# Order of work in a hybrid encoder block: value pairs ahead of their gate pairs, and three steps of background jobs moved by one tick

## The chip, the cores and the metric

One core of a Trainium2 chip runs the whole kernel in one launch. The metric is the device time in microseconds. TensorE (PE, with PEld for its weight loads), VectorE (DVE), ScalarE (ACT), GpSimd (POOL) and SyncE (SP) run side by side, each through its own list of instructions in order; they meet at semaphores. DMAs are issued from the queues of SP, ACT and POOL.

## The reference, cut to what matters

```python
h = rms_norm(x, pre_norm_w)                       # x: 2048 x 1024, float32
proj = h @ w_in                                   # 1024 x 7168
hy_in, hy_gate, sg_u, sg_v, sg_gate = split(proj)
x0, x1, v = split(short_conv_centred(hy_in, conv_w, conv_b))   # 3 taps
k = hyena_filter(...)
y_a = x0 * long_conv_bidir(v * x1, k, hyena_skip) * silu(hy_gate)   # by FFT in the reference
vn = layer_norm(sg_v, per head of 128) * sgu_norm_w + sgu_norm_b
mixed = einsum('hpq,bnqhd->bnphd', sgu_w, chunks(vn)) + sgu_b       # 8 heads, chunks of 128 rows
y_b = sg_u * mixed * silu(sg_gate)
out = x + rms_norm(concat(y_a, y_b) @ w_out, post_norm_w)
```

## The kernel before

**Foreground.** `Body.stream` computes the two projections as 72 "pairs" of 128-column blocks, each pair by a 2 x 2 block scheme with seven products (units 0 to 6) instead of eight. A unit is `product`: 12 matmuls of 128 x 128 by 512 columns into a PSUM bank `proj` (lines 304 to 306; operands are split into a high and a low part, so each product takes three matmuls). The moving operand of unit u is the tile `x_u` (buffer numbers in a listing tell the units apart), the weights are `wu`, made of `wraw` and `ws` by `prep_begin` (L606 to L614) and `prep_unit` (L631 to L637), one pair ahead. In the PE's order a pair runs unit 0, then units 5 and 6 of the pair before (`finish_pair`), then its own units 1 to 4. `snap` copies a bank to SBUF on ACT (`sn`, L648), `add` sums two banks' worth on DVE (L652).

**Kinds of pairs.** The rows are done in two halves (h = 0, 1). `self.order` is B(0) + U(0) + GV(0) + U(1) + GV(1) + B(1) + O(0) + O(1). A U pair makes two inputs of the long convolution, a G pair its gate and x0, a V pair (value pair) the `sg_v` columns of two heads, a B pair `sg_u` and its gate. There are 8 pairs of each kind, but 4 of V. O pairs are the output projection, 8 for each half of its inner dimension. GV(h) stands as G, G, V four times over. The stages, each with its own pool and its own background source, are: B(0); U(0); GV(0); U(1); GV(1) + B(1); O(0); O(1).

**Background.** What follows a projection is a generator, a "job": `go` runs it to its first `yield` and puts it on the list `active`; `tick` runs every job on the list by one step. `run` ticks at every second unit. A job that is put on the list during a tick gets its next step in that same tick, because the loop reaches the appended entry. `staggered` starts one job of a list per step.

- `u_job` (U pairs): two short convolutions (`conv`: ACT L879, DVE L880, L881), for h = 1 the product `ut` (DVE L914), then four `u1_job`s: four transposes of `ut` into bank `a` (PE L924), `uh`, `ul` (ACT L926, DVE L928), twelve matmuls into banks `b`, copies and two stores `AU<-ev` on the ACT queue each.
- `v_job` (V pairs, one for each of the two heads): loads `sw` and `bi` on the SP queue, one matmul with `ones` (PE L962, DVE L963) and two `mix_job`s: transposes of `v` (PE L980), per-row statistics and normalisation on DVE (L984, L985, L988, `vn` at L992) with a root on ACT (L987), then four matmuls with `sw` (PE L997) and the result back into `v` (DVE L1000). After that, for h = 1, one store `VM<-v` on SP; for h = 0 a load of `ug`, two products (DVE L1005) and two stores on SP.
- `o_job` (O(1) pairs, two output rows' blocks each): adds the part of O(0) (DVE L1129), sums squares on ACT (L1131, one instruction over 1024 columns into `part`), scales on DVE (L1132), root and reciprocal (L587, L589), final sum (DVE L1134) and the store on SP.
- `load_x` replaces the seven `x_u` at a change of half: one load on SP, casts on ACT (L558), subtractions on DVE (L559).

A scheduler of the framework sets the final order on each engine from the written order, the dependences and its own estimate of when each instruction can start; so a step that is written elsewhere comes out interleaved with the matmuls of other units.

Of the kernel before, what the change touches and what calls it, by code (L numbers as in the profile page):

```python
# [22 lines left out]
NJ = 16  # L23
# [102 lines left out]
class TakeU(Take):  # L126
# [11 lines left out]
    def c12(self, C, u2):  # L138
        self.b.add(self.r1[:, 9:17].rearrange("q j p -> q (j p)"), C, u2)
        self.b.go(self.b.u_job(self.h, self.c, self.r1, self.rv))  # L140
# [52 lines left out]
class TakeV(Take):  # L193
# [16 lines left out]

    def c12(self, C, u2):
        self.b.add(self.put(self.v0, 1), C, u2, self.view)
        for n, vr in enumerate((self.v0, self.v1)):
            self.b.go(self.b.v_job(self.h, self.c + n, vr))


class TakeO(Take):
# [28 lines left out]
class Body:  # L246
# [77 lines left out]
    def build(self):  # L324
        with ExitStack() as st:
            self.pp = st.enter_context(self.pool("pp", space=PSUM))
            self.dp = st.enter_context(self.pool("dp", space=DRAM))
            self.cp = st.enter_context(self.pool("cp"))
            dram = lambda n, s, dt=F32: self.dp.tile(s, dt, name=n)
            self.AU = dram("AU", [256, NJ, D])  # L330
            self.AK = dram("AK", [256, NJ, D])
            self.KF = dram("KF", [2, 32, 128, 512])
            self.BY = dram("BY", [256, NJ, D])
            self.XG = dram("XG", [NJ, 128, 8, 128])
            self.UG = dram("UG", [8, 128, D])
            self.VM = dram("VM", [8, 128, 8, 128])
            self.U0 = dram("U0", [8, 128, D])
            self.Y = dram("Y", [NJ, 128, 16, 128])
            self.WT = dram("WT", [2, 7, 128, 4, 512])
            self.PT = dram("PT", [NJ, 128, D])  # L340
            self.RB = dram("RB", [D])
            self.GD = dram("GD", [NJ, 128, 2, 128])
            self.XS = dram("XS", [7, 128, 4, 512])
            self.load_consts()
            self.xp = st.enter_context(self.pool("xp"))
            U = lambda h: [(h, "U", c, 8 + c, 16 + c) for c in range(8)]
            G = lambda h: [(h, "G", c, c, 24 + c) for c in range(8)]
            B = lambda h: [(h, "B", c, 48 + c, 32 + c) for c in range(8)]
            V = lambda h: [(h, "V", c, 40 + c, 41 + c) for c in range(0, 8, 2)]
            GV = lambda h: [p for n in range(4) for p in G(h)[2 * n:2 * n + 2] + V(h)[n:n + 1]]  # L350
            O = lambda r: [(r, "O", m, 2 * m, 2 * m + 1) for m in range(8)]
            self.order = B(0) + U(0) + GV(0) + U(1) + GV(1) + B(1) + O(0) + O(1)
            self.at, self.prev, self.to_spill = 0, None, []
            self.WS = {p[1:3]: dram(f"WS{p[1]}{p[2]}", [len(SPILL), 128, 2, 512]) for p in self.order[:28]}
            self.seen = set()
            self.wp = st.enter_context(self.pool("wp"))
            with self.pool("rp") as self.rp:
                with self.pool("xs") as xs:
                    self.x_phase(xs)
                with self.pool("sg") as self.fp:  # L360
                    self.nw_ = 3
                    with self.pool("mlp") as ml:
                        self.mlp(ml)
                    with self.pool("k1") as kp:
                        self.background(self.k1_jobs(kp), 1.4)
                        self.run(self.stream(8))
                        self.rest()
                with self.pool("fa") as self.fp:
                    self.nw_, self.nf = 4, 8
                    self.background(self.x_jobs(1), 0.25)  # L370
                    self.run(self.stream(8))
                    self.rest()
                self.nc.sync.dma_start(self.rc, self.RB.rearrange("(c q) -> q c", c=8))
                with self.pool("fd") as self.fp:
                    self.nw_, self.nf, self.nl = 5, 2, 3
                    self.background(self.kfft_jobs(), 0.85)
                    self.run(self.stream(12, 1))
                    self.rest()
                with self.pool("fb") as self.fp:
                    self.nw_, self.nf = 4, 3  # L380
                    self.f1 = self.fp.tile([128, 2, 2, 128], F32R, name="f1")
                    self.nc.gpsimd.dma_start(self.f1, self.i["c_f1"])
                    self.background(self.wo_jobs(), 0.32)
                    self.run(self.stream(8))
                    self.rest()
                with self.pool("fc") as self.fp:
                    self.nw_, self.nf, self.nl = 4, 6, 4
                    self.background(self.fft_jobs(), 1.0)
                    self.run(self.stream(20, "w0"))
                with self.pool("fo") as self.fp:  # L390
                    self.nw_ = 4
                    self.pw = self.fp.tile([128, D], F32, name="pw")
                    self.nc.scalar.dma_start(self.pw, self.i["post_norm_w"].partition_broadcast(128))
                    self.run(self.stream(8, "w1"))
                    self.run(self.stream(8))
                    self.drain()
# [499 lines left out]
    def u_job(self, h, c, r1, rv):  # L896
        nc = self.nc
        t1 = self.wide([128, 1024], "t1")
        if h:
            us = [self.fp.tile([128, 8, 2, 64], F32, name="ut", bufs=3) for _ in range(2)]  # L900
            for n in range(2):
                nc.sync.dma_start(us[n][:, :, 0], self.U0[c, :, n * 512:(n + 1) * 512].rearrange("q (j p) -> q j p", j=8))
        self.conv(t1, r1, 8 + c, h)
        yield
        t2 = self.wide([128, 1024], "t2")
        self.conv(t2, rv, 16 + c, h)
        if h == 0:
            nc.vector.tensor_tensor(t1, t1, t2, op=ALU.mult)
            nc.sync.dma_start(self.U0[c], t1)
            return  # L910
        for n in range(2):
            sl = slice(n * 512, n * 512 + 512)
            v1, v2 = [t[:, sl].rearrange("q (j p) -> q j p", j=8) for t in (t1, t2)]
            nc.vector.tensor_tensor(us[n][:, :, 1], v1, v2, op=ALU.mult)  # L914
        nc.vector.tensor_tensor(us[1][:, 7, 0, 63:64], self.fix[:, 8 + c:9 + c], self.fix[:, 16 + c:17 + c], op=ALU.mult)
        yield
        self.go(self.staggered([self.u1_job(c, n, us[n // 2]) for n in range(4)]))

    def u1_job(self, c, n, ut):
# [35 lines left out]
    def v_job(self, h, hd, vr):  # L955
        nc, i, fp = self.nc, self.i, self.fp
        sw = fp.tile([128, 128], F32, name="sw", bufs=2)
        nc.sync.dma_start(sw, i["sgu_w"][hd])
        bi = fp.tile([128, 128], F32, name="bi", bufs=2)
        nc.sync.dma_start(bi, i["sgu_b"][hd].partition_broadcast(128))  # L960
        ps = self.bank("a")
        nc.tensor.matmul(ps[:, :128], self.ones, sw, start=True, stop=True)  # L962
        nc.vector.scalar_tensor_tensor(bi, ps[:, :128], self.nb[:, hd:hd + 1], bi, op0=ALU.mult, op1=ALU.add)  # L963
        for n in range(2):
            self.go(self.mix_job(hd, n, vr, sw, bi))
            yield
        yield
        if h:
            nc.sync.dma_start(self.VM[hd], vr.rearrange("d b j p -> d b (j p)"))
            return  # L970
        ug = self.two("ug")
        nc.sync.dma_start(ug, self.UG[hd].rearrange("q (n c) -> q n c", n=2))
        for n in range(2):
            self.gated(h, hd, n, vr, ug[:, n])
# [149 lines left out]
    def o_job(self, j, y, part, done):  # L1124

        nc, fp = self.nc, self.fp
        xr = fp.tile([128, D], F32, name="xr", bufs=3)
        nc.sync.dma_start(xr, self.i["x"].rearrange("(p j) d -> j p d", j=NJ)[j])
        nc.vector.tensor_tensor(y[:, done:], y[:, done:], part[:, done:], op=ALU.add)  # L1129
        ss = fp.tile([128, 1], F32, name="ss", bufs=2)  # L1130
        nc.scalar.activation(part, y, AF.Square, accum_out=ss)  # L1131
        nc.vector.tensor_tensor(y, y, self.pw, op=ALU.mult)  # L1132
        rs = self.rstd(fp, ss)
        nc.vector.scalar_tensor_tensor(y, y, rs, xr, op0=ALU.mult, op1=ALU.add)  # L1134
        nc.sync.dma_start(self.out.rearrange("(p j) d -> j p d", j=NJ)[j], y)
        return
        yield


# [30 lines left out]
```

## Time and profile before

| | |
|---|---|
| median of 3 runs | 2086.94 us (2083.53 to 2091.46) |
| the profiled execution: its own time / its span | 2081.43 us / 2079.6 us |
| PE busy | 1907.2 us, 92% |
| DVE busy | 1347.8 us, 65% |
| ACT busy | 855.0 us, 41% |
| POOL busy | 446.3 us, 21% |
| granted TensorE clock, mean | 0.975 |
| HBM traffic | 250 GB/s over the span |

A row of a table by windows has the window in us from the span's start, its length, then busy us and instruction count of PE, PEld, DVE, ACT and POOL, the granted TensorE clock, the busy share of the DMA engines and GB/s. A row of the waits has engine, line, what released it, total us, times, longest us. A row of the timeline has start, us, engine, line, operation, out<-in, shapes, and in brackets the idle time before it with what ended it.

### The profile page before, as it was taken

What the parts mean: (1) busy time and instruction counts of PE and PEld (TensorE: products, weight loads), DVE (VectorE), ACT (ScalarE), POOL (GpSimd) and SP (SyncE); (2) the same over time, 40 slices, a digit from 0 to 9 for tenths busy, and PEclk for the clock granted to TensorE, in tenths of its full rate; (3) what the DMA queues carried; (4) which work ended last, traced back from release to release, by engine and by line L of the source; (5) the groups of instructions that cost most, each with busy time, mean ns of one, the idle gap of its engine ahead of it and who ended that gap; (6) DMA issues with size and microseconds to landing.
All of it is one profiled execution on the core that took longest, in us unless ns stands there. A gap on an engine that the chain in (4) does not pass through costs nothing. (4 is left out here: it accounts for less than half of the span.)

```text
span 2079.6 us, 23943 instructions
## 1 busy us (share of the span) xinstructions
PE 1907.2 (92%) x7832; PEld 1419.1 (68%) x7832; DVE 1347.8 (65%) x2070; ACT 855.0 (41%) x1538; POOL 446.3 (21%) x392
## 2 busy tenths in 40 slices
PE   4689999999999999888999999989999999999997
PEld 3465666777777766666777666656677777887776
DVE  6767878787655545655544888887773226436876
ACT  6344444565434443534444223322322224335443
POOL 3431322233222121111111101101011112323331
PEclk9899999999999999999999999989999999999999
DMA  8388777786779796897786888878978888536563
GB/s 265 110 265 268 238 261 253 227 274 230 247 258 297 259 315 208 327 274 236 256 276 194 294 271 265 282 237 274 302 244 307 282 269 282 194 102 243 192 212 132
DMA packets 330203, 515.89 MB, mean 248 GB/s; under 512 B 107451, under 2 KB 177339, under 8 KB 327359
## 3 DMA queue, kind: packets, MB, share of 16 engines
q1 hardware_dynamic: 263328, 439.58, 64.9%
q10 hardware_dynamic: 61856, 69.81, 9.8%
q0 software_dynamic: 4896, 4.98, 1.0%
q8 instruction: 62, 1.02, 0.2%
q14 instruction: 61, 0.50, 0.1%
HBM read 316.10 MB, written 204.48 MB: 250 GB/s over the span
## 5 line engine op out<-in xcount | busy, mean ns | idle before, releaser
L304 PE MATMUL proj<-x,wu 128*128 128x512 f32 x2016 | 834.9, 415 | 36.0 <-ACT sn L648 15.1
L305 PE MATMUL proj<-x,wu 128*128 128x512 f32 x2016 | 808.2, 401 | 10.6 <-DVE wu L637 8.8
L306 PE MATMUL proj<-x,wu 128*128 128x512 f32 x2016 | 806.6, 400 | 1.2 <-DVE x L559 0.6
L304 PEld LDWEIGHTS proj<-x,wu 128*128 128x128 f32 x2016 | 383.6, 190 | 146.2 <-issue 32.8
L637 POOL TENSOR_TENSOR wu<-wraw,wu 128x512 fp32r<-128x512 f32 x172 | 257.3, 1497 | 1038.1 <-ACT wu L635 855.5
L305 PEld LDWEIGHTS proj<-x,wu 128*128 128x128 f32 x2016 | 383.7, 190 | 113.3 <-issue 24.9
L306 PEld LDWEIGHTS proj<-x,wu 128*128 128x128 f32 x2016 | 383.2, 190 | 94.6 <-issue 12.7
L635 ACT CAST wu<-wraw 128x512 fp32r<-128x512 f32 x216 | 133.5, 619 | 281.6 <-PE proj L306 240.3
L637 DVE TENSOR_TENSOR wu<-ws,wu 128x512 fp32r<-128x512 f32 x176 | 129.7, 739 | 156.0 <-ACT wu L635 155.6
L635 ACT CAST wu<-ws 128x512 fp32r<-128x512 f32 x176 | 108.6, 620 | 220.3 <-PE proj L306 160.3
L648 ACT COPY sn<-proj 128x512 f32<-128x512 f32 x216 | 125.6, 581 | 108.4 <-PE proj L306 80.3
L614 POOL TENSOR_TENSOR ws<-wraw 128x512 f32<-128x512 f32 x44 | 79.0, 1795 | 174.5 <-DVE wu L637 111.7
L1073 DVE TENSOR_TENSOR pa<-b,k 64x512 f32<-64x512 f32 x128 | 87.4, 683 | 40.6 <-PE b L1070 29.8
L614 POOL TENSOR_TENSOR ws<-wraw,ws 128x512 f32<-128x512 f32 x44 | 59.5, 1353 | 223.4 <-DVE wu L637 210.1
L1073 DVE TENSOR_TENSOR pb<-b,k 64x512 f32<-64x512 f32 x128 | 88.8, 694 | 1.8
L614 DVE TENSOR_TENSOR ws<-wraw 128x512 f32<-128x512 f32 x44 | 39.6, 901 | 71.3 <-DMA wraw<-in_w_in_dram 39.2
L1082 PE MATMUL b<-pa,tb 128*128 128x512 f32 x128 | 71.7, 645 | 15.1 <-DVE pa L1077 5.5
L1084 ACT COPY ev<-b 128x512 f32<-128x512 f32 x64 | 37.4, 587 | 99.4 <-PE b L1082 88.8
L559 DVE TENSOR_TENSOR x<-x 128x1024 fp32r<-128x1024 f32 x42 | 56.3, 1381 | 19.2 <-ACT x L558 19.2
L1033 PE MATMUL b<-raw,tk 128*128 128x512 f32 x128 | 62.9, 612 | 5.5 <-issue 4.8
L862 PE MATMUL b<-s,ff 128*128 128x512 f32 x128 | 62.2, 603 | 4.4 <-ACT ev L864 2.9
L1070 PE MATMUL b<-raw,tu 128*128 128x512 f32 x128 | 63.2, 604 | 1.7 <-DMA raw<-AU 1.7
(170 smaller groups left out, 2230.5 us busy)
## 6 DMA issues: line engine op xcount, KB each, us to landing
wraw<-in_w_in_dram SPq DMA_DIRECT2D x84, 512.0 KB, 4.9
WSB<-wu SPq DMA_DIRECT2D x32, 512.0 KB, 4.8
dd<-in_c_dec_dram SPq DMA_DIRECT2D x32, 512.0 KB, 5.6
AK<-ev ACTq DMA_DIRECT2D x64, 256.0 KB, 4.5
WSU<-wu SPq DMA_DIRECT2D x32, 512.0 KB, 4.5
WSG<-wu SPq DMA_DIRECT2D x32, 512.0 KB, 5.0
raw<-AK SPq DMA_DIRECT2D x32, 512.0 KB, 6.9
KF<-ev ACTq DMA_DIRECT2D x32, 512.0 KB, 6.0
```

The source lines that it names most:

```text
L304: t.matmul(ps, sh, mh, start=first, stop=False, **kw)
L305: t.matmul(ps, sl, mh, start=False, stop=False, **kw)
L306: t.matmul(ps, sh, ml, start=False, stop=last, **kw)
L614: eng.tensor_tensor(t, x, y, op=op)
L635: nc.scalar.copy(w[:, 0], src[u])
L637: eng.tensor_tensor(w[:, 1], src[u], w[:, 0].bitcast(F32), op=ALU.subtract)
L648: self.nc.scalar.copy(s, ps)
L862: nc.tensor.matmul(ps, self.ff[:, d], s[d], start=True, stop=True)
L1033: nc.tensor.matmul(ps, tv[:, n], raw[:, n], start=True, stop=True)
L1070: nc.tensor.matmul(u, tv[0][:, n], raw[:, n], start=True, stop=True)
L1073: nc.vector.tensor_tensor(o, uu, kk, op=ALU.mult)
L1082: nc.tensor.matmul(ps, tv[1][:, n], prod[n], start=True, stop=True)
```

## The change

Four edits, all of order; each operation stays as it is.

1. GV(h) becomes V, G, G four times over: each value pair runs ahead of the two gate pairs that it followed.
2. A value pair's two `v_job`s are started through `staggered`, so the second head starts one step after the first; and `v_job` loses one empty `yield` ahead of its last step (the store of `VM`, or the load of `ug` and the products).
3. `u_job` gets one more `yield` ahead of the transposes of `ut`.
4. `o_job` gets a `yield` between the sum (L1129) and the sum of squares, except for the last two blocks of rows.

```diff
     def c12(self, C, u2):
         self.b.add(self.put(self.v0, 1), C, u2, self.view)
-        for n, vr in enumerate((self.v0, self.v1)):
-            self.b.go(self.b.v_job(self.h, self.c + n, vr))
+        self.b.go(self.b.staggered([self.b.v_job(self.h, self.c + n, vr) for n, vr in enumerate((self.v0, self.v1))]))
...
-            GV = lambda h: [p for n in range(4) for p in G(h)[2 * n:2 * n + 2] + V(h)[n:n + 1]]
+            GV = lambda h: [p for n in range(4) for p in V(h)[n:n + 1] + G(h)[2 * n:2 * n + 2]]
...
         nc.vector.tensor_tensor(us[1][:, 7, 0, 63:64], self.fix[:, 8 + c:9 + c], self.fix[:, 16 + c:17 + c], op=ALU.mult)
         yield
+        yield
         self.go(self.staggered([self.u1_job(c, n, us[n // 2]) for n in range(4)]))
...
         for n in range(2):
             self.go(self.mix_job(hd, n, vr, sw, bi))
             yield
-        yield
         if h:
...
         nc.vector.tensor_tensor(y[:, done:], y[:, done:], part[:, done:], op=ALU.add)
+        if j < NJ - 2:
+            yield
         ss = fp.tile([128, 1], F32, name="ss", bufs=2)
...
-        return
-        yield
```

Line numbers of the changed kernel are one lower than those of the kernel before over most of the file (the matmuls of a product are L303 to L305 there, the sum L651, `ut` L913, the split of `x` L558).

**The PE's order at the first turn of `u` in stage U(1).** The numbered `x` tiles tell the units: before, `x_6735` is that of unit 3 and `x_6759` that of unit 4. Before:

```order
L304 MATMUL proj<-x_6735,wu 128x512
L305 MATMUL proj<-x_6735,wu 128x512
L306 MATMUL proj<-x_6735,wu 128x512
L924 MATMUL a<-ident,ut 128x128 x8
L304 MATMUL proj<-x_6759,wu 128x512
L305 MATMUL proj<-x_6759,wu 128x512
L304 MATMUL b<-uh,f_6951 128x512
```

In the changed kernel `x_6720` is the tile of unit 0 and `x_6909` that of unit 5:

```order
L304 MATMUL proj<-x_6720,wu 128x512
L305 MATMUL proj<-x_6720,wu 128x512
L303 MATMUL proj<-x_6720,wu 128x512
L304 MATMUL proj<-x_6720,wu 128x512
L924 MATMUL a<-ident,ut 128x128 x8
L305 MATMUL proj<-x_6720,wu 128x512
L303 MATMUL b<-uh,f_6951 128x512
```

The eight transposes stood at the end of unit 3 of the next pair, 37 matmuls of `proj` behind the unit that ends the `u` pair, and stand now at the end of unit 0 of the pair after it, 60 matmuls behind. For the eight pairs of the stage this distance was 37, 50, 29, 46, 41, 46, 35, 36 matmuls and is now 60, 61, 49, 61, 49, 61, 50, 33.

**DVE's order at the first value pair of GV(0).** `v` are the value tiles of the two heads, `ws` a sum of weights for the next pair that reads the load `wraw`. Before:

```order
L652 TENSOR_TENSOR v_4702<-proj,sn 128x8x8x8
L637 TENSOR_TENSOR wu<-ws,wu 128x512 x2
L614 TENSOR_TENSOR ws<-wraw 128x512
L614 TENSOR_TENSOR ws<-ws,wraw 128x512
L652 TENSOR_TENSOR v_4623<-proj,sn 128x8x8x8
L963 SCALAR_TENSOR_TENSOR bi<-a,nb,bi 128x128
L984 BN_STATS bs<-a 128x6 x2
```

In the changed kernel:

```order
L651 TENSOR_TENSOR v_4330<-proj,sn 128x8x8x8
L636 TENSOR_TENSOR wu<-ws,wu 128x512 x2
L651 TENSOR_TENSOR v_4269<-proj,sn 128x8x8x8
L613 TENSOR_TENSOR ws<-wraw 128x512
L613 TENSOR_TENSOR ws<-ws,wraw 128x512
L983 BN_STATS bs<-a 128x6 x2
```

Here the last sum of `v`, for which the transposes wait, went from behind the two `ws` to ahead of them, and the statistics stand behind them. At the second, third and fourth value pair of GV(0) the two `ws` stand ahead of the last sum of `v` in the changed kernel; before, that was so at the first, second and third.

**DVE's order at the seam from GV(0) to U(1)**, where the seven `x` tiles are replaced. Before (`v_6679`, `v_6757` are the heads of the last value pair):

```order
L559 TENSOR_TENSOR x_6681<-x_6681 128x1024 x2
L652 TENSOR_TENSOR v_6757<-proj,sn 128x8x8x8
L963 SCALAR_TENSOR_TENSOR bi<-a,nb,bi 128x128
L559 TENSOR_TENSOR x_6705<-x_6705 128x1024 x2
L652 TENSOR_TENSOR v_6679<-proj,sn 128x8x8x8
L559 TENSOR_TENSOR x_6735<-x_6735 128x1024 x2
L984 BN_STATS bs<-a 128x6 x2
```

In the changed kernel (`r_6807`, `sg` and `t` belong to the last gate pair, `r_6992` to the first U pair):

```order
L558 TENSOR_TENSOR x_6809<-x_6809 128x1024 x2
L651 TENSOR_TENSOR r_6807<-proj,sn 128x512
L558 TENSOR_TENSOR x_6833<-x_6833 128x1024 x2
L879 SCALAR_TENSOR_TENSOR t<-r_6807,cw,t 128x1024
L558 TENSOR_TENSOR x_6863<-x_6863 128x1024 x2
L880 SCALAR_TENSOR_TENSOR t<-r_6807,cw,t 128x1024
L947 SCALAR_TENSOR_TENSOR sg<-sg,rc,t 128x1024
L558 TENSOR_TENSOR x_6888<-x_6888 128x1024 x2
L558 TENSOR_TENSOR x_6909<-x_6909 128x1024 x2
L558 TENSOR_TENSOR x_6939<-x_6939 128x1024 x2
L651 TENSOR_TENSOR r_6992<-proj,sn 128x512
```

The statistics and normalisation of two heads stood among the splits of `x` and went two pairs ahead; a gate pair's four instructions stand there instead, and all splits are now ahead of the first sum of U(1).

## The prediction

> **What bounds the kernel now.** I read the page first, then the windows by stage, then the waits of PE in each stage, then the timeline around the longest waits.
>
> ```profile
> span 2079.6 us, 23943 instructions
> PE 1907.2 (92%) x7832; PEld 1419.1 (68%) x7832; DVE 1347.8 (65%) x2070; ACT 855.0 (41%) x1538; POOL 446.3 (21%) x392
> ```
>
> PE is busy for 1907.2 of 2079.6 us. Order cannot remove a matmul, so what the change can win is part of the 172 us in which PE stands still, and time at a lower clock behind a stop. The windows below are GV(0), the seam with U(1), GV(1), the rest of that stage, and the two O stages.
>
> ```profile
> 530.00:857.00 327.00, 311.85 (x1294) 233.43 (x1294) 175.42 (x344) 146.01 (x273) 70.53 (x64) 0.98 0.83 274
> 857.00:1112.00 255.00, 224.56 (x1002) 180.01 (x1001) 143.45 (x221) 113.48 (x215) 39.16 (x41) 0.95 0.83 261
> 1112.00:1537.00 425.00, 405.16 (x1551) 270.21 (x1550) 332.53 (x579) 136.07 (x236) 50.35 (x45) 0.98 0.84 271
> 1747.00:2080.00 333.00, 308.99 (x1343) 252.09 (x1342) 214.97 (x259) 140.48 (x240) 95.29 (x62) 0.98 0.54 185
> ```
>
> The seam and U(1) have the most idle time for their length, 30.4 of 255 us, and the lowest clock, 0.95; the idle times of the others are 15.2, 19.8 and 24.0 us. The waits of PE say for what. Rows of 889 to 1142, then of 530 to 889, then of 1906 to 2080:
>
> ```profile
> PE a L924 <- DVE ut L914: 17.5, 7, 5.3
> PE b L304 <- ACT uh L926: 2.0, 1, 2.0
> PE b L306 <- DVE ul L928: 1.8, 2, 1.4
> PE proj L304 <- ACT sn L648: 0.6, 1, 0.6
> ...
> PE a L980 <- DVE v L652: 7.6, 3, 3.0
> PE b L997 <- DVE vn L992: 6.8, 2, 6.5
> ...
> PE proj L304 <- ACT sn L648: 5.8, 6, 1.0
> ```
>
> A stop costs twice. Below, a stop and the stretch behind it, three times, and the slow stretch behind the longest stop.
>
> ```profile
> 908.00:912.00 4.00, 0.00 (x0) 0.00 (x0) 3.96 (x4) 0.62 (x2) 1.55 (x1) 1.00 0.91 282
> 912.00:916.00 4.00, 3.39 (x13) 3.06 (x14) 3.27 (x6) 0.91 (x4) 1.37 (x3) 0.57 0.74 250
> ...
> 1034.00:1038.00 4.00, 1.54 (x13) 1.08 (x11) 4.00 (x5) 1.21 (x5) 1.42 (x3) 1.00 0.09 30
> 1038.00:1042.40 4.40, 4.40 (x14) 3.27 (x13) 2.20 (x4) 1.99 (x4) 0.23 (x1) 0.61 0.48 122
> ...
> 605.00:608.60 3.60, 1.61 (x10) 0.97 (x9) 2.69 (x6) 2.23 (x3) 0.66 (x1) 1.00 0.98 297
> 608.60:612.00 3.40, 3.40 (x12) 2.71 (x11) 1.11 (x8) 0.30 (x1) 0.00 (x0) 0.50 0.92 346
> ...
> 875.00:881.60 6.60, 3.06 (x13) 3.06 (x14) 6.19 (x17) 0.07 (x1) 1.82 (x1) 0.50 0.49 183
> ```
>
> After a stop of 2 us or more the clock is granted by half for 3.4 us: 4.0 us at 0.57, 4.4 at 0.61 and 3.4 at 0.50 each lose 1.7 us of matmul time.
>
> **The change part by part.**
>
> *Turns of `u` a step later.* The rows show the first wait, what DVE did before it, and how fast PE walks:
>
> ```profile
> 906.21 0.39 PE L306 MATMUL proj<-x,wu 128*128 128x512 f32 x1
> 906.43 0.39 PE L304 MATMUL proj<-x,wu 128*128 128x512 f32 x1
> 912.61 0.69 PE L924 MATMUL a<-ident,ut 128*128 128x128 f32 x2 [5.34 <-DVE ut L914]
> 949.34 1.00 PE L924 MATMUL a<-ident,ut 128*128 128x128 f32 x6 [4.60 <-DVE ut L914]
> 1037.15 0.55 PE L924 MATMUL a<-ident,ut 128*128 128x128 f32 x3 [2.46 <-DVE ut L914]
> 1121.89 0.66 PE L924 MATMUL a<-ident,ut 128*128 128x128 f32 x4 [0.92 <-DVE ut L914]
> ...
> 900.65 1.31 DVE L581 TENSOR_TENSOR t<-wo_raw 128x512 f32<-128x512 f32 x1 [7.91 <-DMA wo_raw<-in_w_out_dram]
> 908.35 2.29 DVE L881 SCALAR_TENSOR_TENSOR t<-r,cw,t 128x1024 f32<-128x1024 f32 x1
> 911.87 1.29 DVE L914 TENSOR_TENSOR ut<-t,t 128x512 f32<-128x512 f32 x2
> ...
> 907.70 1.86 POOL L637 TENSOR_TENSOR wu<-wraw,wu 128x512 fp32r<-128x512 f32 x1 [6.28 <-ACT wu L635]
> ...
> L880 DVE SCALAR_TENSOR_TENSOR t<-r,cw,t 128x1024 f32<-128x1024 f32 x6 | 7.7, 1284 | 6.1 <-ACT t L879 6.1
> ```
>
> A matmul of `proj` starts every 0.22 to 0.23 us. By the distances in the order (37, 50, 29, 46, 41, 46, 35, 36 matmuls before; 60, 61, 49, 61, 49, 61, 50, 33 now) the transposes come later by 5.2, 2.5, 4.5, 3.4, 1.8, 3.4, 3.4 and, at the last pair, -0.7 us of PE's own work. Of the waits 5.34, 4.60, 2.46 and 0.92 (first, second, fifth, eighth pair) this leaves 0.1, 2.1, 0.7 and 1.6, of the rest nothing: 4.5 of 17.5, so 13.0 us go. Of the stage's four slow stretches (the first and the third stand above, the others are at 950 and 1069) one stays, behind the 2.1: 3 x 1.7 = 5.1. Together 18.1 us. What is late next: `uh`, `ul` and `sn`, now 4.4 us together, stand right behind the transposes, and DVE in this stage is itself held by loads of `wo_raw` (7.91 us in one piece), which a faster PE does not bring forward. I let these waits double and take back 4: 14 us. Ends: 0, if all of it reappears there, and 18. The moved step issues eight stores `AU` per pair on the ACT queue; its DMAs go later behind the same copies, and nothing reads `AU` until the next stage. On SP and POOL it issues nothing. The slot of `ut` is held a step longer, but in the order its last transposes still stand ahead of the second next pair's loads.
>
> The operation L881 beside POOL's subtraction took 2.29 us, where L880 on the same shape takes 1.28. The Trainium skill, page SBUF — State Buffer, section Who interferes with whom, has it that a DVE instruction with two SBUF inputs and a reading GpSimd one exclude each other for the whole instruction; by it this one waits until 909.56 and lasts 2.49, near the 2.29 measured. By the row the term stays 14; by the rule, if every such pair met, it would be what the first rival gives.
>
> *Value pairs first, second head later: GV(0).* The last value pair's statistics collide at the seam with the splits of `x`; that is the 6.51 us below and the 6.6 us at half clock, 3.3 lost. In the new order a gate pair's work stands there. From the rows, a value pair costs DVE (21.9 + 16.0 + 11.9 + 9.8) / 4 = 14.9 us in these four groups, a gate pair (9.5 + 7.7) / 6 = 2.9 in its own product (L947) and the first of two like convolution steps (L880).
>
> ```profile
> 878.54 0.79 PE L997 MATMUL b<-sw,vn 128*128 128x128 f32 x2 [6.51 <-DVE vn L992]
> 891.46 1.40 PE L304 MATMUL proj<-x,wu 128*128 128x512 f32 x2 [2.40 <-DVE r L652]
> ...
> L992 DVE TENSOR_SCALAR vn<-a,mv,rs 128x128 f32<-128x128 f32 x64 | 21.9, 402 | 0.1
> L984 DVE BATCH_NORM_STATS2 bs<-a 128x6 f32<-128x128 f32 x64 | 16.0, 277 | 5.5 <-PE a L980 5.5
> L1000 DVE SCALAR_TENSOR_TENSOR v<-b,nw,bi 128x512 f32<-128x512 f32 x16 | 11.9, 741 | 4.9 <-PE b L997 4.8
> L985 DVE BATCH_NORM_AGGREGATE mv<-bs 128x2 f32<-128x6 f32 x64 | 9.8, 163 | 0.0
> L947 DVE SCALAR_TENSOR_TENSOR sg<-sg,rc,t 128x1024 f32<-128x1024 f32 x6 | 9.5, 1582 | 0.0
> ...
> 690.15 1.15 DVE L614 TENSOR_TENSOR ws<-wraw 128x512 f32<-128x512 f32 x1 [4.46 <-DMA wraw<-in_w_in_dram]
> 691.94 0.68 DVE L652 TENSOR_TENSOR v<-proj,sn 128x512 f32<-128x512 f32 x1
> ```
>
> So 6.5 + 3.3 = 9.8 us go; the 2.40 behind them I leave, since the splits still stand ahead of the first sum. But the same pair now meets the wait of the others: its sum of `v` stands behind a `ws` that waits for `wraw`, and costs 7.6 / 3 = 2.5 and 1.7 of clock, 4.2. The first value pair loses that wait (the sum is ahead of `ws` now), yet its statistics stand behind it, so `vn` is late by about as much: 0. The term is 9.8 - 4.2 = 5.6; ends -4.2 (the seam's wait only moves) and 9.8 + 2.4 + 3.7 - 4.2 = 11.7. The second head's loads `sw` and `bi` on SP come later with it and are read later; the last step of `v_job` comes a step earlier, its load of `ug` or store of `VM` too, ahead of which nothing on SP is due.
>
> *GV(1).* DVE is busy for 332.5 of 425 us, PE waits 19.8 in all, and the pairs are the same in another order. I take 0; the ends are the gain of an equal 5.6 and the second rival.
>
> *Sums of squares.* Their step is later in the written order, but on ACT the square stays right ahead of the `sn` copy for which PE waits 1.0 us a pair; the sum on DVE moves ahead of a 1.28 us operation in about half the pairs. 1.5 us, between 0 and all 5.8. No DMA but the output's store moves, and the last pair's chain is untouched.
>
> *Sum*: 14 + 5.6 + 0 + 1.5 = 21 us. Against the profiled execution, 2081.43 us (its span and 1.8 around it): 2060. That execution lies 5.5 below the median of the runs, 2086.94; against the median, 2066.
>
> **The rivals.** *The turns run into POOL.* With PE no longer standing, DVE's four operations of 1.28 us per pair and POOL's subtractions meet each time and take 2.3. That is 4 us a pair, more than the 3 us by which the transposes moved on average; the term of 14 falls to 0, and the time is 2086.94 - 7 = 2080. For it: the 2.29 at the first pair; against it: POOL has 39 us of work in 255.
>
> *The value pairs meet the transform in GV(1) (slower).* The second head's start falls into the same tick as the first head's second half, so DVE has two heads stacked at one place, while it is at 78% with the transform's products. If at each of the four value pairs PE waits for one head's statistics, 14.9 / 2 = 7.5 us and 1.7 of clock, that is 37 us: 2103. It decides from 21 / 4 = 5.3 us a pair; below, the kernel is still not slower. For it: the 6.51 at the seam, where DVE was loaded as much. Against: the work is the same as before, and PE has transform matmuls to run meanwhile.
>
> *It does not do what it says.* The scheduler places instructions by readiness, the second head starts about 20 matmuls later and the square not at all; if the seam's wait only moves, the turns alone count: 14 - 4.2 = 10, so 2077.
>
> **How the numbers follow.** No change and a change of 0.5%, 10.4 us, is about what a measurement of this kernel can tell apart: faster is below 2076.5, slower above 2097.4. The forecast, with its terms between half and their upper ends, 0.63, all of it faster. POOL 0.11 and the step without effect 0.12 are both within 0.5%. GV(1) 0.14: slower. The range: the upper ends together, 18 + 11.7 + 5.8 = 35.5, and the same again of the 5.6 in GV(1), give 2046; at the top both rivals within 0.5% and the median with no gain, 2087. Outside lie the slower rival and a little below. The likeliest case alone has 2048 to 2076.
>
> **What would show it.** Each step: PE's wait at L924 falls from 17.5 to about 4, and the clock of U(1) rises from 0.95; the 6.5 at L997 near the seam is gone; four waits of about 2.5 at L980 or L997 in GV(0) instead of three; the O stage's `sn` waits stay near 1.0. It is wrong if PE's idle time in U(1) stays at 30 us under other names, or if idle time in GV(1) rises above 30.

## The result and the profile after

The changed kernel took 2071.64 us (median of 6 runs, 2066.04 to 2078.3); the kernel before took 2084.71 us beside it (6 runs, 2082.41 to 2091.46). The ratio is 0.9936, with an interval of 0.9915 to 0.9956: 13 us faster, where 21 were forecast (2066 of 2086.94 is 0.990, outside the interval). Direction and range held; the size did not: the largest term was too large, and a stage that stood at nothing became longer. Of all executions here, two ran some 4% longer at a granted clock of 0.84 (2173.88 us of the squares alone, 2158.52 us of turns, heads and five slots); the ratios leave them out, the medians count them.

The profiled execution took 2072.21 us, its span 2070.2. Its page begins:

```profile
span 2070.2 us, 23947 instructions
PE 1904.2 (92%) x7832; PEld 1414.1 (68%) x7832; DVE 1345.9 (65%) x2070; ACT 857.4 (41%) x1540; POOL 452.0 (22%) x392
```

The work of each engine is what it was; the time came from PE standing still less. The windows of the stages (GV(0); the seam with U(1); GV(1); the O stages, all shifted a little, since the stages begin at other times now):

```profile
530.00:860.00 330.00, 317.58 (x1350) 238.46 (x1349) 187.83 (x402) 147.50 (x274) 71.00 (x64) 0.98 0.83 274
860.00:1098.00 238.00, 214.26 (x943) 169.41 (x942) 130.23 (x163) 110.02 (x210) 38.98 (x41) 0.97 0.86 273
1098.00:1531.00 433.00, 410.59 (x1594) 275.13 (x1592) 336.24 (x630) 143.42 (x246) 50.39 (x44) 0.98 0.83 265
1740.00:2070.00 330.00, 307.55 (x1337) 250.83 (x1335) 213.20 (x257) 138.76 (x237) 99.17 (x62) 0.99 0.54 185
```

In the seam and U(1) PE now stands still for 23.7 us (238.00 less 214.26) instead of 30.4, at a granted clock of 0.97 instead of 0.95; in GV(1) for 22.4 instead of 19.8. PE's waits, of U(1), of GV(0), of the seam alone (860 to 889.8) and of O(1):

```profile
PE b L303 <- ACT uh L926: 10.3, 6, 2.6
PE b L305 <- DVE ul L928: 3.3, 5, 1.0
PE a L924 <- DVE ut L913: 2.4, 1, 2.4
...
PE a L979 <- DVE v L651: 8.3, 3, 3.1
...
PE proj L303 <- ACT r L871: 4.1, 1, 4.1
PE proj L303 <- ACT sn L647: 2.7, 1, 2.7
...
PE proj L303 <- ACT sn L647: 3.7, 4, 1.0
```

The wait for `ut` is gone as forecast (17.5 to 2.4; of the 17.5, 0.9 stood at the start of GV(1), where the changed kernel has no such wait), but `uh` and `ul` hold PE for 13.6 us where they held it for 3.8. The 6.51 us at the normalised rows is gone from the seam, but the first products of U(1) wait there for `sn` and `r`, 6.8 us.

The table splits one profiled execution of each kernel at the first matmul of a stage (84 matmuls into `proj` make a pair; "seam" is the first pair of U(1)). In brackets stand PE's idle time and the time at half clock, in us; of the latter, half is lost. A kernel with "`x` kept" leaves out the exchange of `x` at the seam (see below). Each row is one execution, and a stage that no edit touches varies too: B(0) took 309.5 to 315.5 us in these fourteen.

| kernel | GV(0) | seam | rest of U(1) | GV(1) + B(1) | span |
|---|---|---|---|---|---|
| before | 327.4 (15.1/14) | 38.8 (9.3/10) | 215.3 (21.1/14) | 635.1 (20.2/14) | 2079.6 |
| after | 329.0 (12.4/10) | 29.7 (6.8/7) | 206.8 (16.9/7) | 641.6 (22.8/17) | 2070.2 |
| turns alone | 327.1 | 40.8 | 206.0 (14.8/11) | 636.2 | 2075.1 |
| order of pairs alone | 340.8 | 28.0 | 213.7 | 636.3 | 2085.0 |
| heads alone | 323.1 | 40.0 | 216.1 | 626.5 (15.5/3) | 2070.4 |
| squares alone | 325.1 | 38.5 | 219.3 | 634.0 | 2081.4 |
| after, five slots | 329.7 | 29.3 | 194.0 (5.5/0) | 636.5 | 2047.4 |
| before, five slots | 326.9 | 38.9 | 201.7 (12.1/7) | 632.1 | 2063.4 |
| turns and heads | 325.1 | 40.1 | 209.1 (16.2/14) | 626.4 | 2061.3 |
| after, value pairs first in GV(0) alone | 329.7 | 30.6 | 205.3 (14.8/10) | 627.9 (12.9/7) | 2055.2 |
| the same, five slots | 328.8 | 29.4 | 196.0 (6.4/3) | 626.9 | 2045.4 |
| turns and heads, five slots | 326.7 | 36.4 | 200.0 (10.6/3) | 631.2 | 2058.4 |
| before, `x` kept | 328.2 | 25.5 (0.0/0) | 221.2 | 632.9 | 2072.6 |
| after, `x` kept | 330.5 | 19.0 (0.0/0) | 203.0 | 637.5 | 2053.8 |

By this table the span's 9.4 us come from GV(0) with the seam -7.5, the rest of U(1) -8.5, GV(1) with B(1) +6.5, both O stages -0.9, and all stages ahead of GV(0) +0.9.

### The profile page after: what moved, and what is told of

It reads as the page before. It is cut to its first block, busy times and chain, and to the rows that moved or that the text cites. A ratio compares the mean times of both kernels' runs of the same rounds, so it can differ in the third digit from the quotient of the medians.

```text
span 2070.2 us, 23947 instructions
## 1 busy us (share of the span) xinstructions
PE 1904.2 (92%) x7832; PEld 1414.1 (68%) x7832; DVE 1345.9 (65%) x2070; ACT 857.4 (41%) x1540; POOL 452.0 (22%) x392
## 4 chain that ended last, share of the span: by engine, by line
PE 33%; DVE 8%; DMA 6%; issue 2%; ACT 1%; POOL 1%; SPq 0%; DVEq 0%; ACTq 0%; POOLq 0%
PE proj L305 8%; PE proj L304 8%; PE proj L303 8%; PE b L1081 3%; PE b L1107 2%; PE b L1069 2%; DMA x<-WT 1%; DVE pb L1072 1%; DVE pa L1072 1%; DMA wraw<-Y 1%; DMA WT<-t 1%; DVE x L558 1%; DVE pa L1076 1%; PE b L996 1%; DVE wu L636 1%
## 5 line engine op out<-in xcount | busy, mean ns | idle before, releaser
L303 PE MATMUL proj<-x,wu 128*128 128x512 f32 x2016 | 833.0, 414 | 35.7 <-ACT sn L647 13.2
L304 PE MATMUL proj<-x,wu 128*128 128x512 f32 x2016 | 810.8, 402 | 12.8 <-DVE wu L636 10.3
L305 PE MATMUL proj<-x,wu 128*128 128x512 f32 x2016 | 807.6, 401 | 1.1 <-DVE x L558 0.6
L636 POOL TENSOR_TENSOR wu<-wraw,wu 128x512 fp32r<-128x512 f32 x172 | 262.3, 1525 | 1047.5 <-ACT wu L634 819.1
L303 PEld LDWEIGHTS proj<-x,wu 128*128 128x128 f32 x2016 | 383.6, 190 | 143.6 <-issue 33.7
L305 PEld LDWEIGHTS proj<-x,wu 128*128 128x128 f32 x2016 | 383.4, 190 | 94.5 <-issue 13.5
L651 DVE TENSOR_TENSOR r<-proj,sn 128x512 f32<-128x512 f32 x64 | 43.8, 685 | 40.4 <-PE proj L305 39.6
```

The source lines that it names most:

```text
L303: t.matmul(ps, sh, mh, start=first, stop=False, **kw)
L304: t.matmul(ps, sl, mh, start=False, stop=False, **kw)
L305: t.matmul(ps, sh, ml, start=False, stop=last, **kw)
L636: eng.tensor_tensor(w[:, 1], src[u], w[:, 0].bitcast(F32), op=ALU.subtract)
```

## Each edit alone

Turns of `u` a step later, and nothing else:

```diff
         yield
+        yield
         self.go(self.staggered([self.u1_job(c, n, us[n // 2]) for n in range(4)]))
```

> The kernel before with the extra step ahead of the turns of u alone. Theory one (the account behind the forecast): PE's wait at L924 falls from 17.5 us to about 4, the waits for uh and ul grow to about 13, U(1) itself is about 9 us shorter, and of that 2 to 3 us come back at the start of GV(1), where the last turns now run: 5 to 9 us faster in all. Rival: the late turns delay the value pairs and the transform behind them, GV(1) is longer by what U(1) wins: within 2 us of the kernel before.

Measured: 2070.31 us against 2082.26, ratio 0.9950 (0.9930 to 0.9971). U(1) behind its first pair falls by 9.3 us, and PE waits there 3.5 us for `ut` and 9.9 for `uh` and `ul`. The first theory came, with a gain a little above its 5 to 9 us.

The order of the pairs, and nothing else:

```diff
-            GV = lambda h: [p for n in range(4) for p in G(h)[2 * n:2 * n + 2] + V(h)[n:n + 1]]
+            GV = lambda h: [p for n in range(4) for p in V(h)[n:n + 1] + G(h)[2 * n:2 * n + 2]]
```

> The kernel before with V ahead of its two G in both halves, alone. Theory one: the seam's wait of 6.5 us at L997 and its 3.3 us of slow clock go, the stage GV(0) is 2 to 4 us longer, GV(1) unchanged: 5 to 8 us faster. Rival: in GV(1) the value pairs lie two pairs earlier, where DVE is loaded by the transform, and GV(1) with B(1) takes 6 us more: within 3 us of the kernel before.

Measured: 2086.66 us, ratio 1.0019 (1.0001 to 1.0037): a little slower. The seam falls from 38.8 to 28.0 us, but GV(0) grows from 327.4 to 340.8; about 6.5 us of both are the last value pair's own matmuls, which went from the one to the other. Neither theory came: the gain did not, and GV(1) with B(1), 636.3 us, is not longer by the rival's 6 either.

The second head a step later (`staggered`, and the empty `yield` of `v_job` removed), and nothing else:

> The kernel before with the second head a step later and the empty step of a value pair's job gone, alone. Theory one: nothing that PE waits for moves by more than a microsecond, the time is within 3 us of the kernel before. Rival: the stacked heads are what lengthens GV(1) in the changed kernel: 4 to 7 us slower, in GV(1).

Measured: 2074.97 us, ratio 0.9971 (0.9956 to 0.9986). GV(0) loses 4.3 us, GV(1) with B(1) loses 8.6. Neither theory came: one had no change, the other a slower GV(1).

The squares a step later, and nothing else:

> The kernel before with the step ahead of the sums of squares alone. Theory one: the six waits of 1.0 us for sn in O(1) fall to 5.4 in all, as in the changed kernel: 0 to 1 us faster, which these runs cannot tell from nothing. Rival: the trace of the changed kernel hides a gain of some us by another cause; then 3 us or more.

Measured: 2082.32 us, ratio 1.0005 (0.9988 to 1.0023): no change clear of the noise. The waits of O(1) changed as in the changed kernel: `sn` fell, and the next one took most of it. Waits of before and of this kernel from 1906 to the end:

```profile
PE proj L304 <- ACT sn L648: 5.8, 6, 1.0
PE proj L305 <- DVE wu L637: 1.9, 1, 1.9
...
PE proj L304 <- ACT sn L648: 3.7, 4, 1.0
PE proj L305 <- DVE wu L637: 3.4, 3, 1.9
```

The sum of both is 7.7 us before and 7.1 here. Of the four edits two pay, one pays nothing, and the one that stands first in the change, the order of pairs, costs when it is alone; the four ratios multiply to 0.9945, and 0.9936 was measured for all together.

## Where the gain of the turns went: slots

PE waits in U(1) for `uh`, a copy on ACT. The question is what ACT waits for. ACT's waits of the changed kernel in U(1), DVE's there, and two of ACT's copies from the timeline:

```profile
ACT uh L926 <- DMA WT<-t: 8.6, 4, 4.5
ACT uh L926 <- DVE t L580: 4.5, 2, 3.3
...
DVE t L580 <- DMA WT<-t: 15.4, 6, 4.1
...
DVE ul L928 <- DMA WT<-t: 9.2, 5, 3.8
...
1031.94 0.58 ACT L926 CAST uh<-a 128x512 fp32r<-128x512 f32 x1 [3.27 <-DVE t L580]
1090.05 0.59 ACT L926 CAST uh<-a 128x512 fp32r<-128x512 f32 x1 [4.50 <-DMA WT<-t]
```

`uh` reads bank `a`, and neither `WT` nor `t` is its data. They are the tiles and stores of the weight job that runs in the background of this stage. Its differences `t` (L580) and `uh`, `ul` come from one ring of buffers (the helper `self.f`), and this stage gives the ring three. A copy to `uh` must wait until a store `WT<-t` has left the slot that it gets; `ul` waits for the same stores. In the changed kernel, `uh` falls on them more often: ACT's two waits come to 13.1 us, before to 4.7 (3.4 and 1.3). If that is so, more slots end it:

```diff
                 with self.pool("fb") as self.fp:
-                    self.nw_, self.nf = 4, 3
+                    self.nw_, self.nf = 4, 5
```

> The changed kernel with five instead of three slots of the pool's tile f in the stage U(1). Theory (slots): the 10.3 us for which PE waits for uh in the changed kernel come from ACT waiting for a slot that a tile t of the output weights' job still holds until its store WT has landed (8.6 and 4.5 us of ACT's waits); with five slots that wait falls below 4 us and U(1) behind its first pair gets 6 to 9 us shorter than the 206.8 of the changed kernel: about 0.35% faster than it. Rival (queue): ACT is late because its own list of casts and copies is long there; then the wait for uh stays at 8 to 11 us and the time with it.

Measured: 2057.49 us against 2079.74, ratio 0.9893 (0.9868 to 0.9918). U(1) behind its first pair takes 194.0 us instead of 206.8, with 5.5 us idle instead of 16.9. The stage is 12.8 us shorter, where 6 to 9 were expected; the theory of the slots came, the rival's wait of 8 to 11 us did not. PE's waits there, and the window of that stretch:

```profile
PE b L305 <- DVE ul L928: 2.3, 4, 1.4
PE a L924 <- DVE ut L913: 1.9, 1, 1.9
...
884.30:1078.30 194.00, 188.47 (x858) 148.37 (x856) 109.93 (x145) 94.94 (x185) 33.64 (x35) 1.00 0.90 282
```

No row is left for `uh`, and the granted clock is 1.00 over the stretch. `ul` on DVE still waits 7.4 us for stores `WT`, but PE feels only 2.3 of it.

The control is the kernel before with the same edit. There PE waited mostly for `ut`, so the slots should hardly matter:

> The kernel before with five slots in place of three, nothing else. Slot theory: the slots cost PE only what stands at `uh` and `ul`, 3.8 us of waits, since the wait for `ut` (16.5 us) comes first; 0 to 4 us, ratio 0.998 to 1.000. Rival, that more slots are worth the same without the later turns: 0.994 to 0.996.

Measured: 2071.08 us against 2082.59, ratio 0.9949 (0.9929 to 0.9969). This missed what I expected of the slots; the rival's number came. The slots alone are worth as much as the turns alone, and U(1) falls by 13.6 us. The waits of DVE before, in U(1), and the wait of PE for `ut`, before from 889 to 1111 and with five slots:

```profile
DVE t L581 <- DMA WT<-t: 9.6, 7, 2.3
...
PE a L924 <- DVE ut L914: 16.5, 6, 5.3
...
PE a L924 <- DVE ut L914: 12.9, 8, 5.1
```

```profile
944.91 1.09 PE L924 MATMUL a<-ident,ut 128*128 128x128 f32 x8 [1.69 <-DVE ut L914]
```

The first row was in the profile before, and I had not read it: DVE too waits for slots, 9.6 us, with `ut` queued behind it. With five slots that row is gone from DVE's waits, the 4.60 us at the second pair are 1.69, and PE has no row for `uh` and `ul` left. So the same ring held PE in two ways, by DVE ahead of `ut` and by `uh` and `ul`. The first way was the smaller part of the wait for `ut`: 3.6 of 16.5 us went with the slots, and at the first pair 5.11 of 5.34 us stayed. The later turns take away nearly all of that wait, whatever its cause, but they do not shorten the ring's hold: with them DVE's `t` waits 15.4 us for it, not 9.6, and `ul` 9.2, not 4.7. For the whole kernel the ratios multiply (0.9950 by 0.9949 by 0.9971 for the heads is 0.987, which is what the kernel with all three gave, below). In U(1) alone the two gains do not add up in full: 9.3 and 13.6 us apart, 15.3 to 21.3 in the three kernels that have both.

## The seam: the exchange of `x`

The sum had the stop at the seam go with the statistics. To see what the exchange of `x` itself costs, both kernels were run without it. The second half then runs on the first half's columns of `x`; its load, casts and splits are left out.

```diff
-                    self.run(self.stream(12, 1))
+                    self.run(self.stream(12))
```

> The kernel before without the exchange of the seven x tiles at the seam from GV(0) to U(1): the loads, casts and splits there are left out, and U(1) to GV(1) go on with the first half's rows. Theory (the seam is bound by the exchange: DMA at 1.0, DVE's 17.5 us of splits): even with the last value pair behind its gates the first pair of U(1) has less than 2 us of idle PE and takes 27 to 30 instead of 38.8 us. Rival (the value pair's own chain of statistics is too long for the matmuls around it): the wait of about 6 us at L997 stays.

> The changed kernel without the exchange of `x` at the seam: the second half runs on the first half's columns, so the loads, casts and subtractions of `x` there are left out. If the exchange of `x` holds the seam in the changed kernel too: the first pair of U(1) falls from 29.7 us (idle 6.8) to about 21, its waits for `sn` and `r` go, and the span falls by 5 to 9 us unless U(1) gives some back. If the wait for `sn` and `r` there is the order of their own copies: the pair stays near 29 us.

Measured, one profiled execution each: 2074.34 and 2055.86 us. Windows of the first pair of U(1), first the changed kernel, then the kernel before without the exchange, then the changed kernel without it:

```profile
860.00:889.80 29.80, 22.99 (x87) 17.91 (x86) 18.83 (x18) 15.94 (x26) 5.48 (x6) 0.89 0.99 354
...
858.60:884.00 25.40, 25.38 (x135) 20.92 (x134) 18.07 (x65) 6.93 (x16) 4.65 (x6) 1.00 0.57 155
...
862.30:881.30 19.00, 19.00 (x85) 15.76 (x84) 7.06 (x7) 6.35 (x15) 4.58 (x6) 1.00 0.68 210
```

Without the exchange PE never waits there, in either kernel; the wait at L997, which the rival would have kept, is gone too. Before, the pair held 135 PE instructions, now about 86: the 6.5 us between 25.5 and 19.0 are the value pair's own matmuls, which went into GV(0). What the exchange costs the pair is 38.8 - 25.5 = 13.3 us before and 29.7 - 19.0 = 10.7 after. So the stop of the seam was not removed; 2.6 us of it were. It has other names now. DVE's timeline in the changed kernel, where PE stands still until 879.85:

```profile
871.96 7.00 DVE L558 TENSOR_TENSOR x<-x 128x1024 fp32r<-128x1024 f32 x6
878.87 0.68 DVE L651 TENSOR_TENSOR r<-proj,sn 128x512 f32<-128x512 f32 x1
```

All splits stand ahead of the first sum `r`, as the order of the changed kernel had shown, and the DMA engines are busy for 0.99 of the pair.

The kernel before without the exchange gained 13.3 us at the seam but only 7.0 in its span: U(1) gave back 6 and was at half clock for 27 us instead of 14. The changed kernel without it lost 16.4 us of span, where 5 to 9 were expected: 10.7 at the seam, the rest mostly in U(1) (3.8) and GV(1) with B(1) (4.1), no more than an untouched stage varies. Both are single executions, and what they gave back or gained elsewhere was not followed further.

## GV(1): what the order of pairs costs, and what the heads bring

The order of pairs was left new in GV(0) and put back in GV(1):

```diff
-            GV = lambda h: [p for n in range(4) for p in V(h)[n:n + 1] + G(h)[2 * n:2 * n + 2]]
+            GV = lambda h: [p for n in range(4) for p in (G(h)[2 * n:2 * n + 2] + V(h)[n:n + 1] if h else V(h)[n:n + 1] + G(h)[2 * n:2 * n + 2])]
```

> The changed kernel with value pairs first in the first half only; GV(1) stands as before. Theory (earlier value pairs fall into the loaded part of the transform): GV(1) and B(1) together, 641.6 us in the changed kernel, come down by 8 to 13 us, and the time is 0.3 to 0.6% below the changed kernel's. Rival: what lengthens GV(1) there are the late turns that run into it, 641.6 stays within 4 us.

Measured: 2061.58 us against 2079.74, ratio 0.9905 (0.9884 to 0.9927), with GV(1) and B(1) at 627.9 us, 13.7 less than in the changed kernel: the theory came. Beside it the old order in both halves, with turns and heads (the squares old too, which are worth nothing):

> Turns of u and heads as in the changed kernel, but value pairs behind their gate pairs as before, in both halves (squares as before). Theory (the order of pairs loses): the gains of the two edits add, 0.50% and 0.29%: 0.993 to 0.991 of the kernel before, not slower than the changed kernel, with GV(1) at about 413 us. Rival (the edits need each other): heads bring something only with pairs turned round, or the turns take it back in GV(1): 0.996 or more.

Measured: 2062.63 us, ratio 0.9908 (0.9884 to 0.9931): the gains add, and the rival's 0.996 is out.

The traces say it more sharply than the ratios. GV(1) with B(1) takes, with the old order there, 632 to 636 us in five kernels without the heads' edit, and 626 to 631 in five with it. With the new order it takes 636.3 without (one kernel) and 636.5 to 641.6 (three kernels) with it. By the means, 634.1, 627.8 and 638.5, the heads' edit is worth some 6 us there, where the forecast had 0, and the new order takes that back and more, 10.7 us. One place carries it, the second gate pair behind the second value pair. Its window in the kernel before, the changed one, the half order, and the heads alone:

```profile
1344.30:1402.40 58.10, 49.45 (x174) 29.98 (x173) 47.32 (x88) 15.09 (x26) 4.26 (x4) 0.88 0.77 238
...
1262.30:1319.50 57.20, 45.77 (x159) 28.63 (x158) 47.67 (x93) 14.29 (x24) 3.91 (x4) 0.88 0.70 222
...
1328.30:1372.80 44.50, 40.18 (x159) 26.55 (x158) 37.56 (x77) 12.54 (x21) 4.20 (x4) 0.96 0.73 236
...
1345.10:1389.20 44.10, 40.54 (x159) 26.68 (x159) 37.63 (x77) 12.50 (x21) 4.20 (x4) 0.96 0.74 238
```

In the changed kernel DVE does 93 instructions there, 47.67 us, against 77 and 37.56 where only GV(0) has the new order; PE does the same number of instructions in both and is idle for 11.4 us, with its clock at 0.88. Its waits in that window:

```profile
PE b L1081 <- DVE pa L1076: 5.5, 2, 3.4
PE b L996 <- DVE vn L991: 3.9, 2, 3.0
```

`vn` and the transform's `pa` wait for the same engine. The kernel before had that same pile: 88 instructions, and 8.6 us idle, of which the waits put 5.0 down to DVE and 3.6 to nothing that the profile shows. The order alone has it too (53.0 us for that pair, 9.1 idle, but there 4.9 of the waits name a load `tb`). A second head that starts a step later takes the pile apart in the old order and does not in the new one; so in the main the new order undoes the heads' gain there. That DVE's pile holds PE there is read from the rows (9.4 of the 11.4 us in the changed kernel name DVE); which of DVE's instructions brings it back in the new order was not tried by itself.

## The two fastest versions

> The changed kernel with the value pairs first in GV(0) alone, and five slots. Slot theory and order theory (value pairs first pay at the seam and cost in GV(1)): the seam takes 29 to 30 us, U(1) behind it 194, GV(1) with B(1) 627; ratio about 0.984, at or up to 0.2% below the same kernel with the old order in GV(0) too. Rival, that the seam's gain is only work moved into GV(0): the two are equal within 0.1%, 0.985.

Measured, value pairs first in GV(0) alone, with turns, heads, squares and five slots: 2048.1 us against 2082.59, ratio 0.9851 (0.9827 to 0.9874). The seam takes 29.4 us, U(1) behind it 196.0, GV(1) with B(1) 626.9.

> The kernel before with the turns a step later, the second head a step later, and five slots in place of three for the pool in which `uh` and the tiles of the weight job share a ring; old order of pairs, old squares. Slot theory: the U(1) stage behind the seam takes what it took with five slots in the changed kernel (194 us, idle about 5.5) in place of 209 (16.2), so the ratio goes from 0.9908 to about 0.985, 2049 us; GV(1) with B(1) stays at 626 us. Rival, that the new order of pairs is needed for the gain of the slots: 0.990.

Measured, the old order in both halves, with turns, heads and five slots: 2055.0 us, ratio 0.9871 (0.9848 to 0.9893). The two intervals overlap, as those of the two kernels with three slots do, so the order in GV(0) is not shown to pay in the whole. In the traces GV(0) and seam together are 4.9 us shorter with it, in both comparisons (360.3 against 365.2, 358.2 against 363.1). Five slots brought U(1) to 196 and 200 us, where 194 was expected of both; GV(1) with B(1) took 631.2 us in the second, where 626 was. Between the changed kernel (0.9936) and the same with the old order in GV(1) (0.9905), and between the two with five slots (0.9893 and 0.9851), the difference is 0.3 and 0.4%; each pair of intervals overlaps a little, and both say the same.

## Why the prediction was right or wrong, point by point

- **Turns of `u`, -14 forecast.** The step "this leaves 4.5 of 17.5" held: 2.4 were left. The clock came back for less than was counted: 14 us at half clock became 7, so 3.5 us and not 5.1. The prediction's rule for the clock, read from three stops, has exceptions in the same trace: behind stops of 2.26 us (until 357.11) and 2.01 us (until 982.01) the clock stayed at 1.00, behind one of 1.88 us (until 1068.83) it was 0.59 over 4.2 us. In the changed kernel's U(1) only two of the four stops above 2 us were followed by half clock. The step that failed is "I let these waits double and take back 4". `uh` and `ul` went from 3.8 to 13.6 us, 9.8 taken back, because they wait for slots that stores must leave; with five slots 2.3 are left. U(1) behind the seam fell by 8.5 us, of which the row counts (863 PE instructions before, 849 now) put about 3 into GV(1).
- **Value pairs first and heads in GV(0), -5.6 forecast, -7.5 measured.** Near in size by luck, since its working was wrong. "9.8 us go" failed: the exchange of `x` still costs the seam 10.7 of 13.3 us. The price of 4.2 did not come either: GV(0) still has three waits for `v`, 8.3 us, not four, since the first value pair has lost its own, as the order had shown. And neither edit gains this alone. By the means of the kernels in the table that have the exchange of `x`, GV(0) and seam take 365.9 us with neither edit (four kernels), 363.8 with the heads alone (three), 368.8 with the order alone (one) and 359.1 with both (four). So the order gains there only beside the heads' step; the working had no such term, and why they need each other was not followed. The 3.7 in the upper end has no row beside it; 2.0 us of wait at the first value pair and 1.7 of clock come to it.
- **GV(1), 0 forecast, +6.5 measured** with B(1), about 3 of it work from U(1). The step that failed is "the pairs are the same in another order. I take 0": the working took both edits as one; they are two terms, some -6 for the heads and +11 for the order on top of them, by the means above (the order without the heads: +2, one execution).
- **Squares, -1.5 forecast.** PE's waits in O(1) fell from 7.7 to 7.1 us; alone the edit is not to be measured.
- **The rivals.** The POOL rival did not come. The Trainium skill, page SBUF — State Buffer, section Who interferes with whom, has a DVE instruction with two SBUF inputs and a GpSimd one that reads SBUF exclude each other. Had they met in each pair, DVE's convolution steps would have risen towards the rival's 2.3 us. The second step took 1636 and 1568 ns on average in U(1) before and 1520 and 1397 now; one of the first steps rose from 1282 to 1427, the other stayed at 1280. Some still meet, not each pair. The value pairs met the transform in GV(1) by the mechanism that the second rival named, DVE with two loads at one place, but for about 10.7 us in all, 2.7 for each of the four value pairs, below the 5.3 from which it decides. And it was the order that brought it back, not the second head's start, as that rival had it. The third rival was half right: the seam's wait did mostly move, but the rest did not stay without effect.

Rows for the POOL point, DVE's groups in U(1) before and after:

```profile
L881 DVE SCALAR_TENSOR_TENSOR t<-rv,cw,t 128x1024 f32<-128x1024 f32 x7 | 11.5, 1636 | 0.3
L881 DVE SCALAR_TENSOR_TENSOR t<-r,cw,t 128x1024 f32<-128x1024 f32 x7 | 11.0, 1568 | 0.0
...
L880 DVE SCALAR_TENSOR_TENSOR t<-rv,cw,t 128x1024 f32<-128x1024 f32 x7 | 10.6, 1520 | 0.5
L880 DVE SCALAR_TENSOR_TENSOR t<-r,cw,t 128x1024 f32<-128x1024 f32 x7 | 9.8, 1397 | 0.2
```

By its own signs: the wait at L924, the rise of the clock, the end of the 6.5 at the seam, `sn` waits of still 1.0 us in O(1) (four, not six) and an idle time below 30 in GV(1) came; the four waits in GV(0) did not, there are three. Of its signs of being wrong, idle time in GV(1) stayed below 30; in U(1) with the seam PE's idle time fell from 30.4 to 23.7 us, so about three quarters of it did stay, in part under the other names `uh`, `ul`, `sn` and `r`.

## What to carry to other kernels

When a step is moved out of PE's way, read next what the waiting engines themselves wait for: a copy that waits for a store it does not read points to a shared ring that is short of buffers, and two more of them were worth as much here as the move (0.5% each, and the ratios multiply). A stop at a change of data has to be priced with that change taken out; else one sees only which instruction happens to stand behind it. Edits that are sent together are to be measured apart and in pairs: the order of pairs cost time alone and took back in GV(1) what the heads' step had gained there, and in the traces it gained in GV(0) only together with that step, which the forecast had priced at nothing by itself.
